# Stores on another queue, tiles in other memory and a new order at the start of SwiGLU in a one-core transformer layer

## The chip, the cores and the metric

The kernel runs on one core of a Trainium2 chip. The metric is the device time of one execution in microseconds, as the median of several runs. A core has TensorE (PE in the profile, PEld its weight loads), VectorE (DVE), ScalarE (ACT), GpSimd (POOL) and SyncE (SP). Here SP does nothing but issue DMA transfers, in the order of its program; a transfer whose condition isn't met holds those behind it.

## The reference

One layer over 2048 latent tokens and 256 context tokens of width 1024, in float32:

```python
h = modulate(rms_norm(x, g0), shift, scale)           # and the same for ctx
q, k, v, r, gate = split(h @ w_in)                    # gated linear attention, 4 heads, both directions
o = scan_forward(q, k, v, gate) + scan_backward(q, k, v, gate)   # the state starts from ctx
x = x + m2 * rms_norm((head_rms_norm(o) * silu(r)) @ w_out, g1)
h = modulate(rms_norm(x, g2), m3, m4)
a, b = split(h @ ffn_w_in)                            # 2 x 2816 columns
x = x + m5 * rms_norm((silu(a) * b) @ ffn_w_out, g3)
```

## The kernel before

Every float32 matmul is made of three: an operand is split into a high part (a cast on ACT or DVE) and a low part (a subtraction on DVE), and hi x hi, hi x lo and lo x hi are summed in PSUM. The work runs through four stages on TensorE.

**Projections and forward scan (0 to about 808 us).** In groups of 512 tokens the projections q, k, v, r are written to DRAM, while the chunks of 128 tokens before them run through the scan (`gla_stages`). Tb, the state that the context hands to the backward scan, stays in a pool of its own (`tbp`, L67 to L69).

**Backward scan, output projection, second norm (about 809 to 1079 us).** Chunks run from 15 down to 0 through `back(gc)`: b0 loads, and steps the state E (from Tb for chunk 15, L678), b1 adds the backward part and takes the head norm, `on` (L690), b2 transposes and multiplies by silu(r), `rt`, b3 multiplies by w_out (two halves, `py`), b4 takes the norm of y, adds x, stores `l1_d` (L754) and keeps the normed rows `xh`. `load_wo` stages the output weights in a buffer `wof` (L644). With four chunks ready, `h2_units` transposes and modulates them to `hf` and makes the operands of SwiGLU: groups 3 and 1 store theirs as they are (L769); groups 2 and 0 come after them and, for each of four blocks k, load two stored blocks (`bl`, L775, L776), make two more and form four sums, each stored to `T_d` (L778 to L787). The sums of group 2 are on POOL, those of group 0 on DVE. The four units of group 0 are run after the loop (L846, L847).

**Features (about 1079 to 1945 us).** SwiGLU's products are done in 2 x 2 blocks with seven products instead of eight (P1 to P7): operands T of P1 to P7, weight blocks and their sums, and results that are summed again. `load_T` (L855) loads one T tile in four parts and splits each; P1, P2 and P6 lie in pool `hL` on the left of memory, the others in `hR` on the right, where the second stage's pool `sq` (bl, y, xh, hf) was until `p2t.close()`. There are 44 features of the two halves p = 1 and 0: 2 x 22. A `Feat` loads its weights wg and wu (L903, L906), and `product` splits a weight block into `whl` (8 buffers) and runs 12 matmuls (L951) into PSUM X (P1, P6, P5, P3), Y (P2) or Z (P7, P4). In step t of the loop (L998) P1, P2, P6 and P7 of feature t and P5, P4 and P3 of feature t-1 are run. `store` puts results into `S_d`, `combine` forms four more results for each pair. Beside it, `w2_units` loads blocks of the output weights (`wl`, six loads for a pair) and stores sums of them to `W_d`. All loads and all stores are on SP (`st = nc.sync`, L38).

**Output (1955 to 2383 us).** `out_group` runs the seven products again: activations `ar` from `S_d` (L1026), weights `wr` from `W_d` or, raw, from w2 (`wraw`, L1036), each in a ring of 14, first for p = 1, then for p = 0.

What sets the order: the program lists the work; when it is built, a planner goes through it in program order and puts next on each engine's queue what it holds to be ready. The order on a queue is then fixed. A pool opened where another was closed reuses its bytes; with `reuse_waits="tile"` a new tile waits for the old tiles that it overlaps, and for no others.

```python
    for u in pend:
        u()
    p2t.close()
    hR = p3.enter_context(tc.tile_pool(name="hR", bufs=1, reuse_waits="tile", side="right"))
```

Of the kernel before, what the change touches and what calls it, by code (L numbers as in the profile page):

```python
# [34 lines left out]
def trunk(ctx, tc, x, cx, modw, cols, rows, consts, wqkr, wv, wvg, wgate, wout, w1, w2, out):  # L35
# [17 lines left out]
    qb_d = [dram.tile([128, H, 128], F32, name=f"qb_d{c}") for c in range(NC_)]  # L53

# [120 lines left out]
    Tf = gp.tile([128, H, DV], F32, name="Tf")  # L175
    glt = [c1.tile([128, 128], F32R, name=f"glt{i}") for i in range(4)]
# [177 lines left out]
    def gla_stages(g, i, c, first):  # L354
# [26 lines left out]
        def s1():  # L381
            e["ks"], e["qs"] = [], []
            for z in range(2):
# [250 lines left out]
    p2t = ExitStack()  # L634
    sp = p2.enter_context(tc.tile_pool(name="sp", bufs=2, reuse_waits="tile"))
# [14 lines left out]
    def back(gc):  # L650
# [13 lines left out]
        def b0():  # L664
# [22 lines left out]
        def b1():  # L687
            op = e["op"]
            ss = sp.tile([128, H], F32, name="ssh", tag="ssh", bufs=3)
            on = sp.tile([128, H, DV], F32, name="on", tag="on", bufs=2)  # L690
# [51 lines left out]
        def b4(xhs):  # L742
# [11 lines left out]
            st.dma_start(out=l1_d[gc], in_=y)  # L754
# [4 lines left out]
    def h2_units(g, xhs):  # L759
# [11 lines left out]
        def second(k):  # L771
# [21 lines left out]

    order = list(range(NC_ - 1, -1, -1))
# [4 lines left out]
    load_wo(range(0, 4), c2, c2)  # L799
# [23 lines left out]
    for i, gc in enumerate(order):  # L823
# [12 lines left out]
        if gc % 4 == 0:  # L836
            pend += h2_units(gc // 4, xhs[gc // 4][::-1])
    p2.close()
    pT.close()
# [3 lines left out]
    p3 = ExitStack()  # L843
# [7 lines left out]
    hR = p3.enter_context(tc.tile_pool(name="hR", bufs=1, reuse_waits="tile", side="right"))  # L851
    ps3z = p3.enter_context(tc.tile_pool(name="ps3z", bufs=1, space=PSUM, reuse_waits="tile", side="right"))
    T = {}

    def load_T(p, i):  # L855
        pool = hL if i in (P1, P2, P6) else hR
# [138 lines left out]
    for i in CHAIN:  # L995
        load_T(1, i)
# [193 lines left out]
```

## Time and profile before

| | us |
|---|---|
| median of 3 runs | 2390.48 |
| lowest, highest | 2389.45, 2391.05 |
| the profiled execution, its own time | 2384.77 |
| its span, first to last instruction | 2383.0 |
| TensorE busy in the span | 2302.0 |

The profile has the engines' instructions with their start and length, what ended an engine's idle time before an instruction, and the DMA transfers. A matmul's length overlaps that of the next. PEclk is the granted clock of TensorE as a share of 2.4 GHz. SPq rows are DMA issues of SP; the length of a merged row (x4) reaches from the first to the last.

### The profile page before, as it was taken

The page shows a single profiled execution, that of the slowest core. Times are in us where ns is not written, and L with a number is a line of the kernel's source. Part 1 is how long each engine was busy: PE and PEld are TensorE (multiplying, and loading weights), DVE is VectorE, ACT ScalarE, POOL GpSimd, SP SyncE. Part 2 cuts the span into 40 slices and gives each one's busy share as a digit, 9 for nine tenths or more (in the row PEclk, how much of TensorE's full clock was granted, in tenths as well). Part 3 has the DMA queues.
Part 4 walks back from the last instruction along what each step waited for, and adds up shares of the span by engine and source line. Part 5 has one row for each costly group of instructions (what it writes and reads, how often), then busy time and mean ns, then how long its engine had stood idle before and what let it go on. Part 6 is the DMA issues. An engine that isn't in the chain of part 4 may idle for free.

```text
span 2383.0 us, 32426 instructions
## 1 busy us (share of the span) xinstructions
PE 2302.0 (97%) x11546; PEld 1939.9 (81%) x11546; DVE 1557.7 (65%) x2478; ACT 1068.8 (45%) x1947; POOL 186.6 (8%) x274
## 2 busy tenths in 40 slices
PE   8999999999998999897999999999999989999998
PEld 4898898898898878685888888888888868888887
DVE  6756666766658576658776666866666647466554
ACT  3535445445547544335433333533333336554552
POOL 1100000000001033631000000000000000001001
PEclk9999999999999999997999999999999999999999
DMA  8765468565455587758787332633233248559655
GB/s 299 225 208 173 148 197 285 177 210 208 153 191 191 206 274 257 243 186 309 258 264 259 125 111 93 230 102 115 97 106 107 75 149 284 191 192 330 201 181 177
DMA packets 228902, 463.98 MB, mean 195 GB/s; under 512 B 22530, under 2 KB 66178, under 8 KB 228740
## 3 DMA queue, kind: packets, MB, share of 16 engines
q1 hardware_dynamic: 228740, 461.92, 57.3%
q8 instruction: 90, 1.47, 0.3%
q14 instruction: 72, 0.59, 0.1%
HBM read 331.27 MB, written 130.56 MB: 194 GB/s over the span
## 4 chain that ended last, share of the span: by engine, by line
PE 52%; DMA 0%; DVE 0%; SPq 0%; ACT 0%; issue 0%; POOLq 0%; POOL 0%; ACTq 0%
PE X L951 20%; PE Z L951 10%; PE X L1074 10%; PE W L1074 8%; PE Y L951 5%; DMA wraw<-w 0%; DMA T<-T_d 0%; DMA T_d<-hf 0%; DVE sa L984 0%; DVE bl L781 0%; DVE y L1055 0%; SPq L906 0%; DVE t L781 0%; DVE hf L781 0%; DVE a L974 0%
## 5 line engine op out<-in xcount | busy, mean ns | idle before, releaser
L951 PE MATMUL X<-T,whl 128*128 128x512 f32 x2112 | 495.7, 390 | 8.2 <-ACT whl L933 7.1
L951 PEld LDWEIGHTS X<-T,whl 128*128 128x128 f32 x2112 | 396.6, 188 | 91.5 <-ACT whl L933 7.5
L951 PE MATMUL Z<-T,whl 128*128 128x512 f32 x1056 | 256.2, 391 | 9.1 <-ACT T L861 9.1
L1074 PE MATMUL X<-wr,ar 128*128 128x512 f32 x1056 | 242.3, 391 | 10.6 <-ACT wr L1038 10.6
L1074 PEld LDWEIGHTS X<-wr,ar 128*128 128x128 f32 x1056 | 199.2, 189 | 52.8 <-ACT wr L1038 11.1
L951 PEld LDWEIGHTS Z<-T,whl 128*128 128x128 f32 x1056 | 199.3, 189 | 51.6 <-ACT T L861 9.5
L86 PE MATMUL pj<-hhi,whi 128*128 128x512 f32 (+1 forms) x544 | 213.6, 395 | 2.1 <-DVE hhi L75 1.4
L87 PE MATMUL pj<-hlo,whi 128*128 128x512 f32 (+1 forms) x544 | 211.4, 389 | 0.0
L88 PE MATMUL pj<-hhi,wlo 128*128 128x512 f32 (+1 forms) x544 | 210.4, 387 | 0.0
L73 ACT CAST whi<-wf 128x1024 fp32r<-128x1024 f32 x104 | 109.0, 1048 | 192.7 <-PE pj L87 84.4
L1028 DVE TENSOR_TENSOR ar<-ar 128x512 fp32r<-128x512 f32 x154 | 106.2, 691 | 131.1 <-ACT ar L1027 130.6
L76 DVE TENSOR_TENSOR wlo<-wf,whi 128x1024 fp32r<-128x1024 f32 x104 | 126.8, 1220 | 86.5 <-ACT whi L73 81.0
L1074 PE MATMUL W<-wr,ar 128*128 128x512 f32 x792 | 180.5, 389 | 0.0
L1074 PEld LDWEIGHTS W<-wr,ar 128*128 128x128 f32 x792 | 148.7, 188 | 30.8
L1027 ACT CAST ar<-ar 128x512 fp32r<-128x512 f32 x154 | 95.5, 621 | 154.6 <-DMA ar<-S_d 107.0
L86 PE MATMUL pj<-whi,hhi 128*128 128x256 f32 x432 | 125.0, 289 | 6.3 <-DVE gs L292 4.9
L951 PE MATMUL Y<-T,whl 128*128 128x512 f32 x528 | 127.7, 390 | 0.0
L87 PE MATMUL pj<-wlo,hhi 128*128 128x256 f32 x432 | 123.2, 285 | 2.8 <-DVE wlo L76 2.8
L88 PE MATMUL pj<-whi,hlo 128*128 128x256 f32 x432 | 122.7, 284 | 0.0
L87 PEld LDWEIGHTS pj<-hlo,whi 128*128 128x128 f32 x544 | 103.5, 190 | 21.3 <-DVE hlo L76 2.2
L86 PEld LDWEIGHTS pj<-hhi,whi 128*128 128x128 f32 x544 | 103.1, 191 | 21.5 <-DVE hhi L75 1.6
L88 PEld LDWEIGHTS pj<-hhi,wlo 128*128 128x128 f32 x544 | 103.4, 190 | 19.7
(231 smaller groups left out, 4273.7 us busy)
## 6 DMA issues: line engine op xcount, KB each, us to landing
ar<-S_d SPq DMA_DIRECT2D x154, 256.0 KB, 3.0
wf<-wqkr SPq DMA_DIRECT2D x68, 512.0 KB, 3.9
wg<-w SPq DMA_DIRECT2D x44, 512.0 KB, 3.5
wu<-w SPq DMA_DIRECT2D x88, 256.0 KB, 2.7
S_d<-sa SPq DMA_DIRECT2D x88, 256.0 KB, 2.0
wr<-W_d SPq DMA_DIRECT2D x88, 256.0 KB, 3.0
wf<-wv SPq DMA_DIRECT2D x36, 512.0 KB, 3.8
wl<-w SPq DMA_DIRECT2D x66, 256.0 KB, 3.7
```

The costliest lines, as they stand in the source:

```text
L73: nc.scalar.copy(out=hi, in_=src)
L76: nc.vector.tensor_sub(out=lo, in0=src, in1=hi.bitcast(F32))
L86: nc.tensor.matmul(out=ps, lhsT=ahi, rhs=bhi, start=start, stop=False)
L87: nc.tensor.matmul(out=ps, lhsT=ahi, rhs=blo, start=False, stop=False)
L88: nc.tensor.matmul(out=ps, lhsT=alo, rhs=bhi, start=False, stop=stop)
L951: nc.tensor.matmul(out=ps, lhsT=w[:, a, ks], rhs=t[:, k, b, :], start=first and k == 0 and n == 0, stop=k == 3 and n == 2, skip_group_chec ...
L1027: nc.scalar.copy(out=t[:, 0, :], in_=raw)
L1028: nc.vector.tensor_sub(out=t[:, 1, :], in0=raw, in1=t[:, 0, :].bitcast(F32))
L1074: nc.tensor.matmul(out=po[j], lhsT=a[:, x, 128 * j:128 * j + 128], rhs=w[:, z, :], start=first and fp == 0 and n == 0, stop=fp == NFP - 1 ...
```

## The change

1. **Queues.** These stores go from SP's queue to POOL's: all of features (`S_d`) and weight sums (`W_d`), the y of chunks 1 and 0 (`l1_d`), and those of group 0's units to `T_d`.
2. **Memory.** Tb lies among the scan's tiles, is scaled at the last chunk and goes through DRAM (`Tb_d`) to E. The staging of the first four output weights shares the buffers of `on`. T of P1 has a pool `hG` of its own below the second stage's pools; the feature weights' pool w3 lies directly above it, then hL with P2, P6, P7 and P5; only P4 and P3 are on the right, with g1, sa and wl. a1 has 3 buffers instead of 4. In the output stage the rings are cut in two: 4 slots of `ar` lie where T of P1 was, 10 of `wr` above, the rest behind; the two sets of PSUM banks lie on either side.
3. **Order.** T of P1 is loaded in the loop of chunks. Features 0 and 1 start together: P1 P1 P2 P2, then P6 P7 P5 of feature 0 and P6 of feature 1, each followed by one of group 0's four units, then the rest. Z of feature 0 takes a buffer of X.
4. **Output weights.** A pair takes four loads of w2 instead of six.

```diff
+    Tb_d = dram.tile([128, D], F32, name="Tb_d")
-    pT = ExitStack()
-    tbp = pT.enter_context(tc.tile_pool(name="tbp", bufs=1))
-    Tb = tbp.tile([128, H, DV], F32, name="Tb")
...
+    Tb = gp.tile([128, H, DV], F32, name="Tb")
...
                     if gc == NC_ - 1:
                         put_fb(gc, lnDb[:, NC_, :, 1])
+                        for h in range(H):
+                            nc.scalar.activation(out=Tb[:, h, :], in_=Tb[:, h, :], func=AF.Copy, scale=fb[:, gc, h:h + 1])
+                        st.dma_start(out=Tb_d, in_=Tb.rearrange("p h v -> p (h v)"))
...
+    p3 = ExitStack()
+    hG = p3.enter_context(tc.tile_pool(name="hG", bufs=1, reuse_waits="tile"))
     sp = p2.enter_context(tc.tile_pool(name="sp", bufs=2, reuse_waits="tile"))
...
-            w = spool.tile([128, D], F32, name="wof", tag="xt2", bufs=2)
+            w = spool.tile([128, D], F32, name="wof", tag="on" if spool is sp else "xt2", bufs=2)
...
-                for h in range(H):
-                    nc.scalar.activation(out=E[0][:, h, :], in_=Tb[:, h, :], func=AF.Copy, scale=fb[:, gc, h:h + 1])
+                sync.dma_start(out=E[0].rearrange("p h v -> p (h v)"), in_=Tb_d)
...
-            st.dma_start(out=l1_d[gc], in_=y)
+            (nc.gpsimd if gc < 2 else st).dma_start(out=l1_d[gc], in_=y)
...
-            st.dma_start(out=Td[P3][k], in_=b22)
+            (st if g > 1 else nc.gpsimd).dma_start(out=Td[P3][k], in_=b22)
...
-                st.dma_start(out=Td[i][k], in_=out)
+                (st if g else nc.gpsimd).dma_start(out=Td[i][k], in_=out)
...
+    T, T_pool = {}, {P1: hG}
...
-    load_wo(range(0, 4), c2, c2)
+    load_wo(range(0, 4), c2, sp)
...
             pend += h2_units(gc // 4, xhs[gc // 4][::-1])
+        if gc == 3:
+            load_T(1, P1)
     p2.close()
...
+    w3 = p3.enter_context(tc.tile_pool(name="w3", bufs=2, reuse_waits="tile"))
     hL = p3.enter_context(tc.tile_pool(name="hL", bufs=1, reuse_waits="tile"))
-    w3 = p3.enter_context(tc.tile_pool(name="w3", bufs=2, reuse_waits="tile"))
...
-    for u in pend:
-        u()
-    p2t.close()
...
+    T_pool.update({i: hL for i in (P2, P6, P7, P5)})
+
+    def w2_units(fp):
+        b = {}
+
+        def load():
+            for j, nn in ((0, 0), (0, 1), (1, 0), (1, 1)):
+                b[j, nn] = hR.tile([128, 512], F32, name="wl", tag="wl", bufs=4)
+                sync.dma_start(out=b[j, nn], in_=w2[fp + NFP * j, :, 512 * nn:512 * nn + 512])
+
+        def sums(*what):
+            for i, out, x, y, op in what:
+                nc.vector.tensor_tensor(out=b[out], in0=b[x], in1=b[y], op=op)
+                nc.gpsimd.dma_start(out=W_d[i][fp], in_=b[out])
...
-                self.Z = ps3z.tile([128, GT], F32, name="Z", tag="Z", bufs=2)
+                if self.f == 0 and self.p == 1:
+                    self.Z = ps3.tile([128, GT], F32, name="Z", tag="X", bufs=3)
+                else:
+                    self.Z = ps3z.tile([128, GT], F32, name="Z", tag="Z", bufs=2)
...
-                self.a1 = o3.tile([128, GT], F32, name="a1", tag="a1", bufs=4)
+                self.a1 = o3.tile([128, GT], F32, name="a1", tag="a1", bufs=3)
...
-            st.dma_start(out=S_d[self.p][i][self.f % NFP], in_=t)
+            nc.gpsimd.dma_start(out=S_d[self.p][i][self.f % NFP], in_=t)
...
-    for i in CHAIN:
+    n = len(seq)
+    feats = {0: Feat(*seq[0]), 1: Feat(*seq[1])}
+    for i in (P2, P6, P7, P5):
         load_T(1, i)
-    n = len(seq)
-    for t in range(n + 1):
+    for j, i in ((0, P1), (1, P1), (0, P2), (1, P2)):
+        feats[j].product(i)
+    for j, i in ((0, P6), (0, P7), (0, P5), (1, P6)):
+        feats[j].product(i)
+        pend.pop(0)()
+    p2t.close()
+    hR = p3.enter_context(tc.tile_pool(name="hR", bufs=1, reuse_waits="tile", side="right"))
+    ps3z = p3.enter_context(tc.tile_pool(name="ps3z", bufs=1, space=PSUM, reuse_waits="tile", side="right"))
+    T_pool.update({P4: hR, P3: hR})
+    for i in (P4, P3):
+        load_T(1, i)
+    done = {(1, i) for i in CHAIN}
+    for j, i in ((1, P7), (1, P5), (0, P4), (0, P3), (1, P4), (1, P3)):
+        feats[j].product(i)
+    for t in range(2, n + 1):
...
-    r4 = p4.enter_context(tc.tile_pool(name="r4", bufs=1, reuse_waits="tile"))
+    rA = p4.enter_context(tc.tile_pool(name="rA", bufs=1, reuse_waits="tile"))
     y4 = p4.enter_context(tc.tile_pool(name="y4", bufs=1, reuse_waits="tile"))
-    ps4 = p4.enter_context(tc.tile_pool(name="ps4", bufs=1, space=PSUM, reuse_waits="tile"))
+    rB = p4.enter_context(tc.tile_pool(name="rB", bufs=1, reuse_waits="tile"))
+    rC = p4.enter_context(tc.tile_pool(name="rC", bufs=1, reuse_waits="tile"))
+    ps4 = {"W": p4.enter_context(tc.tile_pool(name="ps4", bufs=1, space=PSUM, reuse_waits="tile")),
+           "X": p4.enter_context(tc.tile_pool(name="ps4x", bufs=1, space=PSUM, reuse_waits="tile", side="right"))}
...
+    def slot(tag):
+        i = count[tag] % 14
+        count[tag] += 1
+        first, nf = {"ar": (rA, 4), "wr": (rB, 10)}[tag]
+        pool, sfx, nb = (first, "", nf) if i < nf else (rC, "2", 14 - nf)
+        return pool.tile([128, 2, 512], F32R, name=tag, tag=tag + sfx, bufs=nb)
...
-        t = r4.tile([128, 2, 512], F32R, name=tag, tag=tag, bufs=14)
+        t = slot(tag)
...
-        raw = r4.tile([128, 512], F32, name="wraw", tag="wraw", bufs=4)
+        raw = rB.tile([128, 512], F32, name="wraw", tag="wraw", bufs=4)
```

## Rows read from the trace of the kernel before

**Rows 1.** The page, part 1, the whole span: engine, busy us, share, instructions.

```profile
PE 2302.0 (97%) x11546; PEld 1939.9 (81%) x11546; DVE 1557.7 (65%) x2478; ACT 1068.8 (45%) x1947; POOL 186.6 (8%) x274
```

**Rows 2.** Waits of PE, whole span: total us, times, longest.

```profile
PE X L1074 <- ACT wr L1038: 10.6, 1, 10.6
PE Z L951 <- ACT T L861: 9.1, 1, 9.1
PE X L951 <- ACT whl L933: 7.1, 1, 7.1
```

**Rows 3.** Windows: busy per engine (x instructions), clock, DMA share, GB/s; first row L951 alone.

```profile
1078.70:1955.20 876.50, 843.29 (x3696) 695.30 (x3696) 0.98 0.47 157
...
1078.70:1117.80 39.10, 21.38 (x92) 17.09 (x92) 31.18 (x49) 19.01 (x34) 4.91 (x7) 0.75 0.90 312
1055.00:1078.70 23.70, 23.68 (x112) 19.16 (x110) 11.95 (x18) 10.27 (x22) 8.54 (x10) 1.00 0.66 228
1130.00:1940.00 810.00, 810.00 (x3575) 670.71 (x3574) 534.30 (x837) 307.24 (x538) 0.00 (x0) 1.00 0.43 145
...
1115.00:1120.00 5.00, 2.14 (x4) 1.29 (x5) 4.22 (x7) 2.62 (x5) 0.00 (x0) 0.50 0.98 341
```

**Rows 4.** Timeline of PE, first crossing: start, us, line, operation, idle before.

```profile
1078.29 0.39 PE L88 MATMUL py<-wo_hi,olo 128*128 128x512 f32 x1
1085.76 1.22 PE L951 MATMUL X<-T,whl 128*128 128x512 f32 x2 [7.09 <-ACT whl L933]
...
1091.13 4.67 PE L102 MATMUL tp<-ident,xh 128*128 128x128 f32 x24 [0.52 <-DVE xh L95]
...
1117.86 5.21 PE L951 MATMUL Z<-T,whl 128*128 128x512 f32 x12 [9.08 <-ACT T L861]
```

**Rows 5.** Timeline of SP's queue (DMA issues), first crossing.

```profile
1071.18 1.87 SPq L860 DMA_DIRECT2D T<-T_d  x4
1077.59 0.32 SPq L754 DMA_DIRECT2D l_d<-y  x1
...
1079.80 0.43 SPq L903 DMA_DIRECT2D wg<-w  x1
...
1113.01 9.81 SPq L860 DMA_DIRECT2D T<-T_d  x16
```

**Rows 6.** Timeline of DVE, first crossing.

```profile
1083.96 1.41 DVE L751 SCALAR_TENSOR_TENSOR y<-py,ry,A 128x512 f32<-128x512 f32 x2 [0.44 <-POOL ry L82]
...
1110.14 0.69 DVE L781 TENSOR_TENSOR bl<-bl,t 128x512 f32<-128x512 f32 x1
```

**Rows 7.** Groups of DVE from 1078.7 to 1111: busy us, mean ns, idle before.

```profile
L862 DVE TENSOR_TENSOR T<-T 128x512 fp32r<-128x512 f32 x10 | 6.3, 682 | 0.0
```

**Rows 8.** The chain that ended last, in order of time: start, us, work.

```profile
1142.19 2.72 PE Y L951 x12
...
1955.23 31.92 PE X L1074 x132
1987.15 29.92 PE W L1074 x132
```

**Rows 9.** Timeline of all engines, second crossing.

```profile
1941.70 2.88 PE L951 MATMUL X<-T,whl 128*128 128x512 f32 x12
...
1946.70 1.77 SPq L979 DMA_DIRECT2D S_d<-sa  x3
...
1949.06 0.41 SPq L1026 DMA_DIRECT2D ar<-S_d  x1
```

**Rows 10.** Groups of POOL, whole span.

```profile
L753 POOL TENSOR_TENSOR y<-y,xt 128x1024 f32<-128x1024 f32 x15 | 36.7, 2450 | 23.0 <-DVE y L751 18.9 <-DMA xt<-x 4.1
...
L781 POOL TENSOR_TENSOR hf<-hf,hf 128x512 f32<-128x512 f32 x4 | 5.8, 1454 | 0.3
```

**Rows 11.** The page, part 6: DMA issues, KB each, us to landing.

```profile
S_d<-sa SPq DMA_DIRECT2D x88, 256.0 KB, 2.0
```

**Rows 12.** Waits of PE from 800 to 870 us.

```profile
PE tp L722 <- DVE on L703: 3.0, 3, 2.1
```

More of the change, by code (lines that the diff above doesn't have):

```diff
@@ L689, in b1 @@
             ss = sp.tile([128, H], F32, name="ssh", tag="ssh", bufs=3)
-            on = sp.tile([128, H, DV], F32, name="on", tag="on", bufs=2)
+            on = sp.tile([128, D], F32, name="on", tag="on", bufs=2).rearrange("p (h v) -> p h v", h=H)
             for hh in range(2):
@@ L792, in h2_units, with load_T @@
         return [lambda k=k: second(k) for k in range(4)]
+    T, T_pool = {}, {P1: hG}
+    def load_T(p, i):
+        t = T_pool[i].tile([128, 4, 2, GT], F32R, name=f"T{i}", tag=f"T{i}", bufs=1)
+        for k in range(4):
+            raw = t[:, k, 1, :].bitcast(F32)
+            sync.dma_start(out=raw, in_=T_d[p][i][k])
+            nc.scalar.copy(out=t[:, k, 0, :], in_=raw)
+            nc.vector.tensor_sub(out=t[:, k, 1, :], in0=raw, in1=t[:, k, 0, :].bitcast(F32))
+        T[i] = t
     order = list(range(NC_ - 1, -1, -1))
@@ L850, in trunk @@
-    p2t.close()
[L851 to L856, printed above, removed]
-        t = pool.tile([128, 4, 2, GT], F32R, name=f"T{i}", tag=f"T{i}", bufs=1)
-        for k in range(4):
-            raw = t[:, k, 1, :].bitcast(F32)
-            sync.dma_start(out=raw, in_=T_d[p][i][k])
-            nc.scalar.copy(out=t[:, k, 0, :], in_=raw)
-            nc.vector.tensor_sub(out=t[:, k, 1, :], in0=raw, in1=t[:, k, 0, :].bitcast(F32))
-        T[i] = t
@@ L865, in w2_units @@
-    def w2_units():
-        hold = {}
-        def wl(fp, half, n):
-            t = o3.tile([128, 512], F32, name="wl", tag="wl", bufs=3)
-            sync.dma_start(out=t, in_=w2[fp + NFP * half, :, 512 * n:512 * n + 512])
-            return t
-        def sub(i, fp, x, y, op=ALU.subtract):
-            nc.vector.tensor_tensor(out=x, in0=x, in1=y, op=op)
-            st.dma_start(out=W_d[i][fp], in_=x)
-            return x
-        def t1(fp):
-            sub(P5, fp, wl(fp, 0, 1), wl(fp, 0, 0))
-        def t3(fp):
-            b12 = wl(fp, 0, 1)
-            b22 = wl(fp, 1, 1)
-            hold[0] = sub(P7, fp, b22, b12)
-        def t2(fp):
-            b11 = wl(fp, 0, 0)
-            hold[0] = sub(P6, fp, b11, hold[0], ALU.add)
-        def t4(fp):
-            sub(P4, fp, wl(fp, 1, 0), hold[0])
-        return [lambda fp=fp, t=t: t(fp) for fp in range(NFP) for t in (t1, t3, t2, t4)]
@@ L895, in trunk @@
-    units = w2_units()
+    T_pool.update({i: hL for i in (P2, P6, P7, P5)})
[9 more added lines that the diff above has]
+                nc.gpsimd.dma_start(out=W_d[i][fp], in_=b[out])
+        return [load, lambda: sums((P7, (1, 1), (1, 1), (0, 1), ALU.subtract), (P5, (0, 1), (0, 1), (0, 0), ALU.subtract)),
+                lambda: sums((P6, (0, 0), (0, 0), (1, 1), ALU.add)), lambda: sums((P4, (1, 0), (1, 0), (0, 0), ALU.subtract))]
@@ L897, in trunk @@
+    units = [u for fp in range(NFP) for u in w2_units(fp)]
     class Feat:
@@ L971, in product @@
             else:
-                g1 = o3.tile([128, GT], F32, name="g1", tag="g1", bufs=1)
+                g1 = hR.tile([128, GT], F32, name="g1", tag="g1", bufs=1)
                 nc.scalar.activation(out=g1, in_=ps, func=AF.Silu)
@@ L1002, in trunk @@
             j = t - lag
-            if not 0 <= j < n:
+            if not j < n or (j, i) in done:
                 continue
@@ L1007, in trunk @@
                 load_T(0, i)
-        if units:
-            units.pop(0)()
-        if t >= 2 and t % 2 == 0:
+        for _ in range(2 if t == 4 else 1):
+            if units:
+                units.pop(0)()
+        if t % 2 == 0:
             feats[t - 1].combine(feats[t - 2])
@@ L1034, in w2_block @@
         half, nn = {P1: (0, 0), P2: (1, 0), P3: (1, 1)}[i]
-        raw = r4.tile([128, 512], F32, name="wraw", tag="wraw", bufs=4)
+        raw = rB.tile([128, 512], F32, name="wraw", tag="wraw", bufs=4)
         sync.dma_start(out=raw, in_=w2[fp + NFP * half, :, 512 * nn:512 * nn + 512])
-        t = r4.tile([128, 2, 512], F32R, name="wr", tag="wr", bufs=14)
+        t = slot("wr")
         nc.scalar.copy(out=t[:, 0, :], in_=raw)
@@ L1059, in out_group @@
         lo, hi = slice(0, 512), slice(512, 1024)
-        X = [ps4.tile([128, 512], F32, name="X4", tag=tx, bufs=4) for j in range(4)]
+        X = [ps4[tx].tile([128, 512], F32, name="X4", tag=tx, bufs=4) for j in range(4)]
         y0 = [y4.tile([128, D], F32, name="y0", tag="y0", bufs=6) for j in range(4)]
@@ L1067, in out_group @@
             if i in (P2, P7):
-                W = [ps4.tile([128, 512], F32, name="W4", tag=tw, bufs=4) for j in range(4)]
+                W = [ps4[tw].tile([128, 512], F32, name="W4", tag=tw, bufs=4) for j in range(4)]
             po = W if i in (P2, P7, P4) else X
```

6 lines of the change are left out of this document (2 added, 4 removed).

## The prediction

> **What bounds the kernel now.** Busy shares come first: TensorE is busy for 97% of the span [rows 1], so a change pays only where it stands still or runs slowly. The list of who waited for whom names the places: three waits of 10.6, 9.1 and 7.1 us, each a single one [rows 2]. All lie where stages meet. Inside the feature stage, from 1130 to 1940 us, TensorE is busy for all 810 us at full clock, DVE for 534, POOL for none, and the DMA share is 0.43 [rows 3]. The reader should see that nothing in those 810 us can be won, only lost.
>
> The crossings are priced from windows. The 876.5 us from 1078.7, where the attention projection ends [rows 4], to 1955.2, where the output stage starts, hold 3696 matmuls [rows 3]. A product of 12 takes 2.72 us [rows 8], so 308 products need 837.8. The 32 transposes in the stretch need about 4 (24 took 4.67 at half clock [rows 4]). That leaves 34.7 us lost: 10.6 in the second crossing and so 24.1 in the first. There 39.1 us contain 17.7 of standstill, and the mean clock is 0.75 [rows 3]. Behind the 9.1 us wait the granted clock is 0.50, 1.2 GHz [rows 3], and the first product takes 5.21 us instead of 2.72 [rows 4]. The output stage starts likewise: 31.92 against 29.92 us for 132 matmuls [rows 8], 2.0 more.
>
> The queues say who is late. SP issues in order. After four T loads at 1071.18 it stands until 1077.59, when the store of y goes out, which waited for POOL's sum; only at 1079.80 comes wg, the first feature weights [rows 5], and TensorE starts at 1085.76 [rows 4]. Four of the seven T tiles have their memory on the right, where the operand sums live: the last sum ends at 1110.83 [rows 6], the T loads follow at 1113.01 [rows 5], and TensorE goes on at 1117.86 [rows 4]. At the second crossing the last product starts at 1941.70, the sums' stores leave SP at 1946.70 and the first load of the output stage at 1949.06 [rows 9], although what it reads was stored hundreds of us before.
>
> **The first crossing after the change.** Three parts act together. The y stores of the last two chunks and all 20 stores of the last operand sums go to POOL, so SP stands no longer before wg. The weights lie where buffers of the backward stage end early, and T of P1 has memory of its own, so both can be loaded and split before 1078.7, while DVE is at half load (11.95 of 23.7 us [rows 3]). The new order then gives TensorE two P1 products at once, which cover the loads of the next T tiles, and ten products before anything needs the right side. The 7.1 us wait goes with its half-clock tail. New waits come:
> - Y's bank is freed by the projection's last scaling, which ends at 1085.4 [rows 6]; two P1 products end at 1078.7 + 5.4 = 1084.1. Cost 1.3.
> - Y has one buffer, and two P2 products now follow each other: DVE must take the first away, one sum of 0.69 [rows 6] and its handshake. Cost 1.
> - T of P4 still waits for the last operand sum. DVE now has 16 T splits there, where before it had 10 [rows 7]: 6 x 0.69 = 4.1, and two weight splits more, 1.4; four splits for the first two features move ahead of 1078.7, minus 2.8. The last sum so ends near 1113.5. Store, T load and split took 7.0 from the last sum to the product; I add 1 for POOL. TensorE could start P4 at about 1121.
>
> Until then it has 10 products and the transposes: 27.2 + 4 + 2.3 of waits reach 1112.2. T of P3 needs only the memory of xh and y, free earlier, so the planner may put both P3 products first: 1117.6. Stall 3.4 to 8.8, middle 6, then 2 for half clock. Loss left: 2.3 + 8 = 10.3 of 24.1, a gain of **13.8**. Bounds: 5 if the sums slip by 9 us more (the old wait of 9.1 once more), 21 if feature 2 fills the gap.
>
> What is queued behind a POOL store? Norm factors, and y sums of earlier chunks. The last y's store waits for the same sum as the norm behind it, so it holds nobody. A store on POOL has no row. From below: free, with the landing of 2.0 us that SP's store has [rows 11]. From above: a POOL pass over a tile twice its size, 2.45 us [rows 10]. I take a pass over the same size, 1.45 [rows 10], since POOL has to write the transfer out itself.
>
> **The feature stage.** 198 stores (154 of features, 44 of weight sums) leave SP for POOL, which is idle there; 22 loads of 256 KB go. At a DMA share of 0.43 that is worth nothing to TensorE. One a1 buffer goes: each lives for some two features of 7 x 2.72 = 19 us, and three suffice. Four combinations share three sa buffers, so the fourth waits for the first's store; 1.45 us more on DVE, idle for a third of the stage, is hidden. Cost 0; the bound above is rival 4.
>
> **The second crossing.** SP has no stores left in the stage, so A5, the rings' first loads and the raw weights wait for memory alone. The first four activation slots lie on T of P1; nine products, 24.5 us, follow the last P1. Raw weights and weight slots lie on T of P2, P6 and P7, all read before the last three products, 8.2 us. The first output product then follows the last feature product directly; of its PSUM banks on the right two are free and two were Z's. Gain 10.6 + 2.0, less 1 for an evacuation in the way: **11.6**. Bounds: 6 if the splits come late, 12.6.
>
> **The start of the backward stage.** Tb is scaled earlier and goes through DRAM: one store and one load of 512 KB more, four ACT instructions moved. The staging of the first output weights shares buffers with "on"; its second pair of loads could hold the first head norm. But these buffers lie on the scan's gate tiles, free before the scan ends, so the loads can start earlier than before. TensorE waits 3.0 us for "on" here now [rows 12]. I take 0, between minus 3 (that wait gone) and plus 3 (doubled).
>
> Sum: 13.8 + 11.6 = 25.4. The profiled execution took 2384.8 (span 2383.0 and 1.8 around it), so 2359.4; it ran 5.7 below the median of 2390.5, against which I forecast 2390.5 - 25.4 = **2365**.
>
> **A rule against it.** SP stood from about 1073 to 1077.6 before a store [rows 5]: the order of the queue cost these 4.5 us, and issuing did not. The Trainium skill's "DMA: Bandwidth & Descriptors", section "Issuing engines are not separate DMA queues", says that transfers from several engines share the same DMA engines, and that a second issuer saves only sequencer time, usually small. By that rule the moved stores would give almost nothing in the first crossing; the trace agrees that the DMA engines are nearly full there, at 0.90 [rows 3], but not that issue time is all that was lost.
>
> **Rivals.**
> 1. The first crossing is bound by transfers. At a share of 0.90 over 39.1 us, T tiles (6 MB), sums (7 MB) and weights move no faster from another queue; DVE too is busy for 31.2 of them [rows 3]. For it: the same bytes have to pass. Against it: the 4.5 us in which SP stood, and T of P1 and the weights of two features, which move ahead. Gain there 2 to 3 instead of 13.8: 2376. This is where that page's rule leads. Chance 0.13.
> 2. The second crossing stays: the planner still puts the rings' loads last, or a slot overlaps a late reader. For it: before, T of P1 was free by 1920 too, and yet its memory was loaded at 1949 [rows 9]. Against it: then 198 stores stood on that queue. Gain 13.8 only: 2377. Chance 0.11.
> 3. Feature 2 covers the rest of the first crossing: gain 21 + 12.6, 2357. Chance 0.07.
> 4. Slower: POOL's stores set the pace of the feature stage. Its 838 us over 198 stores are 4.23 us each. From 4.23 on, a0, a1 and sa come free too late, DVE blocks and TensorE waits for splits; from 4.36 on the 25 us won are gone. At 5 us: 198 x 0.77 = 152, less 25: 2517. Against it: 4.23 is three times the row I took and above the higher bound of 2.45. Chance 0.06. The Trainium skill's "SBUF — State Buffer", section "SBUF: two separate sides", warns that a store from POOL's queue cannot write its descriptors while DVE runs in a two-port mode; no run here shows such a store.
> 5. The change does nothing visible: other waits take the place of both. 2388. Chance 0.03.
>
> **How the numbers follow.** The forecast has 0.60, with a range of its own of 2355 to 2373. The range of 2352 to 2379 takes in rivals 1 to 3 and leaves out 4, 5 and tails. About 0.2% (4.8 us) can be told from no change. Faster: 0.60, 0.11 of rival 1, 0.11 and 0.07: 0.89. Same: 0.02 of rival 1 and 0.03: 0.05. Slower: 0.06.
>
> **What would show it.** Right: no wait above 1.5 us between 1079 and 1112; wg and T of P1 issued before 1078; a wait of 3 to 9 us at the first P4 or P3; ar and raw weights issued before the last feature product; no long wait at the output stage's first matmul and its first 132 in 29.9 us; TensorE at 100% between. Wrong: waits in the feature stage after 1150 (rival 4), a T of P2 that lands after 1085 (rival 1), ar behind the end of the features (rival 2), or more than 6 us of new waits between 800 and 850.

## The result and the profile after

The change made the kernel slower: 2422.15 us median against 2390.77 in the same comparison, ratio 1.0128 (95% interval 1.0111 to 1.0146). The forecast was 2365. The profiled execution took 2423.08 us, its span 2421.3, which is 38.3 more than before. That is more than the 31.4 between the medians, since the profiled execution of before was 5.7 us below its median.

The page, part 1, and from part 3 the queue of POOL's stores (packets, MB, share of 16 engines' span), kernel after:

```profile
PE 2323.6 (96%) x11546; PEld 1948.2 (80%) x11546; DVE 1558.7 (64%) x2478; ACT 1067.6 (44%) x1947; POOL 307.1 (13%) x494
...
q0 software_dynamic: 17728, 58.21, 6.6%
```

Against [rows 1], TensorE has as many matmuls and is busy 21.6 us longer: part of them ran at the lower clock, and part of those in the output stage at a slower pace (below). POOL has 220 instructions more, which are the moved stores; they are a queue of their own now, 58 MB. The list of waits of PE shows new names on top, and the three waits of [rows 2] are gone or short:

```profile
PE X L939 <- DVE a L954: 17.5, 4, 7.0
PE tp L725 <- DVE on L706: 11.3, 6, 8.0
...
PE X L939 <- DVE y L754: 3.5, 1, 3.5
...
PE X L1089 <- DVE wr L1054: 2.5, 1, 2.5
```

The timeline of PE says where they lie:

```profile
839.07 1.12 PE L725 MATMUL tp<-ident,on 128*128 128x128 f32 x4 [8.04 <-DVE on L706]
...
1096.50 2.93 PE L939 MATMUL X<-T,whl 128*128 128x512 f32 x12
1102.92 1.70 PE L939 MATMUL X<-T,whl 128*128 128x512 f32 x4 [3.50 <-DVE y L754]
...
1151.85 6.52 PE L939 MATMUL Z<-T,whl 128*128 128x512 f32 x15 [1.71 <-ACT T L804]
...
1220.26 2.88 PE L939 MATMUL X<-T,whl 128*128 128x512 f32 x12
1227.58 5.49 PE L939 MATMUL X<-T,whl 128*128 128x512 f32 x12 [4.43 <-DVE a L954]
...
1277.39 4.59 PE L939 MATMUL X<-T,whl 128*128 128x512 f32 x12 [6.99 <-DVE a L954]
...
1986.77 0.49 PE L1089 MATMUL X<-wr,ar 128*128 128x512 f32 x1 [1.19 <-ACT wr L1053]
1989.77 31.85 PE L1089 MATMUL X<-wr,ar 128*128 128x512 f32 x131 [2.50 <-DVE wr L1054]
2021.45 30.43 PE L1089 MATMUL W<-wr,ar 128*128 128x512 f32 x132
```

From such timelines each profile can be cut into stages. "Backward" runs from the scan's last matmul to the projection's last. "First crossing" is the time from there to the start of the 21st product, less 20 x 2.72 and 4 for the transposes; "features" what the other 288 products took beyond 2.72 each; "second crossing" the time from the last product's end to the third output matmul, less the 0.4 of two matmuls; "output" the rest.

| us | before | after | difference | fastest version (below) |
|---|---|---|---|---|
| scan, until | 808.8 | 812.5 | +3.7 | 808.6 |
| backward | 269.7 | 284.0 | +14.3 | 274.3 |
| first crossing, lost | 24.1 | 21.8 | -2.3 | 15.4 |
| features, lost | 0.0 | 25.3 | +25.3 | 0.0 |
| second crossing, lost | 11.7 | 4.3 | -7.4 | 4.3 |
| output | 426.4 | 431.2 | +4.8 | 429.4 |

The differences sum to 38.4. The reader should see that both crossings did become shorter and that three other stages pay for it. The scan's end is not read: it lies between 808.6 and 816.2 in the profiles below, though none of the edits made there touches the scan. Whether the change itself, which scales Tb in the scan, costs something there is not shown.

### The profile page after: what moved, and what is told of

It reads as the page before. It is cut to its first block, busy times and chain, and to the rows that moved or that the text cites. A ratio compares the mean times of both kernels' runs of the same rounds, so it can differ in the third digit from the quotient of the medians.

```text
span 2421.3 us, 32503 instructions
## 1 busy us (share of the span) xinstructions
PE 2323.6 (96%) x11546; PEld 1948.2 (80%) x11546; DVE 1558.7 (64%) x2478; ACT 1067.6 (44%) x1947; POOL 307.1 (13%) x494
## 4 chain that ended last, share of the span: by engine, by line
PE 47%; issue 6%; POOL 5%; DVE 3%; DMA 2%; ACT 1%; SPq 0%; POOLq 0%; ACTq 0%; DVEq 0%
PE X L939 16%; PE X L1089 10%; PE Z L939 8%; PE W L1089 7%; PE Y L939 4%; POOL y L756 1%; POOL W_d L875 1%; DMA T<-T_d 1%; DVE rt L727 1%; POOL S_d L967 0%; DVE y L754 0%; DVE op L700 0%; DMA rt<-r_d 0%; PE py L85 0%; DVE ohi L73 0%
## 5 line engine op out<-in xcount | busy, mean ns | idle before, releaser
L939 PE MATMUL X<-T,whl 128*128 128x512 f32 x2112 | 504.0, 394 | 22.5 <-DVE a L954 17.5
L85 PEld LDWEIGHTS pj<-hlo,whi 128*128 128x128 f32 x544 | 103.9, 191 | 21.6 <-DVE hlo L74 2.3
L86 PEld LDWEIGHTS pj<-hhi,wlo 128*128 128x128 f32 x544 | 103.8, 191 | 19.7
```

The costliest lines, as they stand in the source:

```text
L85: nc.tensor.matmul(out=ps, lhsT=ahi, rhs=blo, start=False, stop=False)
L86: nc.tensor.matmul(out=ps, lhsT=alo, rhs=bhi, start=False, stop=stop)
L939: nc.tensor.matmul(out=ps, lhsT=w[:, a, ks], rhs=t[:, k, b, :], start=first and k == 0 and n == 0, stop=k == 3 and n == 2, skip_group_chec ...
```

## Experiments

Each ratio is to runs of the kernel before on the same chip; differences of 3 or 4 us between two of them are inside their intervals.

### The feature stage: queue or bundle

First what is late there. The timeline of DVE, kernel after:

```profile
1224.30 0.69 DVE L874 TENSOR_TENSOR wl<-wl 128x512 f32<-128x512 f32 x1 [4.68 <-DMA wl<-w]
1224.91 0.68 DVE L919 TENSOR_TENSOR whl<-wu,whl 128x512 fp32r<-128x512 f32 x1
1225.51 1.41 DVE L874 TENSOR_TENSOR wl<-wl 128x512 f32<-128x512 f32 x2
1226.84 0.68 DVE L954 TENSOR_TENSOR a<-a,X 128x512 f32<-128x512 f32 x1
```

DVE stands 4.68 us for a load of output weights; behind it in its fixed order is the sum that empties a bank of PSUM (L954), and at 1227.58 TensorE goes on. Behind the three longer of the four waits TensorE runs at 1.2 GHz for some 5 us: the product above takes 5.49 instead of 2.88, and the windows view of after gives 0.50 as granted clock there (last but two columns) and 0.95 over all 200 us:

```profile
1160.00:1360.00 200.00, 182.51 (x771) 149.12 (x771) 134.91 (x215) 63.04 (x112) 42.63 (x79) 0.95 0.59 204
...
1228.00:1233.00 5.00, 5.00 (x13) 3.83 (x13) 4.42 (x8) 2.14 (x4) 1.08 (x2) 0.50 0.93 313
```

That makes the 25.3: 17.5 of waits and some 8 at the lower clock. The load is late because its buffer is still being stored. Waits of SP's queue, 1160 to 1310 us, kernel after:

```profile
SPq L870 <- DMA W_d<-wl: 65.6, 35, 7.1
```

Two things changed there: the store's queue, and the unit, which now loads four blocks into the four buffers that the unit before is storing.

```diff
 # e2_wsum_sp (after, with)
-                nc.gpsimd.dma_start(out=W_d[i][fp], in_=b[out])
+                st.dma_start(out=W_d[i][fp], in_=b[out])
```

> The changed kernel, but only the 44 stores of weight sums go back to the SyncE queue. Theory Q (the queue): the four weight loads of a unit wait for stores of the unit before, which land late from POOL's queue; DVE stands up to 5.7 us on those loads and TensorE behind it, 17.5 us in four waits between 1223 and 1303 plus some 8 us at half clock. Then the waits go: 2396 to 2402. Theory B (the bundle): four loads at once into four buffers that are all still being stored are late from either queue: 2418 to 2426.

Measured: 2401.2 us, ratio 1.0047 (1.0029 to 1.0064): theory Q, and the features lose 4 instead of 25.3. Waits of PE, 1160 to 1310 us, and then those of SP:

```profile
PE X L939 <- DVE a L954: 1.9, 1, 1.9
```

```profile
SPq L870 <- DMA W_d<-wl: 12.6, 17, 2.0
```

```diff
 # e3_units (after, with the units of before, stores from POOL, four buffers)
-    units = [u for fp in range(NFP) for u in w2_units(fp)]
+    units = [lambda fp=fp, t=t: t(fp) for fp in range(NFP) for t in (t1, t3, t2, t4)]
```

> The changed kernel, but the weight sums are made as in the kernel before, in units of one or two loads each (66 loads, not 44), in four buffers, stores still from POOL. Theory B (the bundle): DVE's waits become short again (before: 21 waits, longest 3.6 us, TensorE none) and the four waits of TensorE go: 2396 to 2403. Theory Q (the queue): stores from POOL hold the buffers just as long, waits stay: 2417 to 2428.

Measured: 2415.7, ratio 1.0111 (1.0089 to 1.0134). TensorE's waits stay at 16.0 us in four, the loads wait 81.6 us at SP for stores. DVE's single waits did become short, as the theory of the bundle said, but they are more, and TensorE stands all the same (waits of DVE, 1160 to 1310 us):

```profile
DVE wl L873 <- DMA wl<-w: 44.5, 29, 3.5
```

So it is the queue and not the bundle; the theory of the bundle has fallen. The reverse test puts the moved stores alone onto POOL's queue in the kernel before:

```diff
 # e6_before_pool (before, with)
-            st.dma_start(out=S_d[self.p][i][self.f % NFP], in_=t)
+            nc.gpsimd.dma_start(out=S_d[self.p][i][self.f % NFP], in_=t)
 # likewise W_d, l1_d of chunks 1 and 0, and T_d of group 0's units
```

> The kernel before with nothing changed but the queue: the stores that the change moves go to POOL. Theory: the weight sums, with three buffers there, wait for stores from the other queue and TensorE for them, some 20 us in the feature stage; the second crossing gains up to 10: 2396 to 2412. Rival: before, memory sets both crossings, and the queue alone costs and brings nothing: 2387 to 2393.

Measured: 2406.4, ratio 1.0067 (1.0053 to 1.0082). TensorE waits for the same sum (10.2 us in two, none before), the features lose 16.4 in all, and the second crossing's wait is 10.9 as before: **the queue alone costs 16 us and brings nothing.** Is it POOL, or any queue that isn't the loads' own?

```diff
 # e7_wsum_act (after, with)
-                nc.gpsimd.dma_start(out=W_d[i][fp], in_=b[out])
+                nc.scalar.dma_start(out=W_d[i][fp], in_=b[out])
```

> The changed kernel, but the 44 stores of weight sums are issued by ScalarE, on a queue that is neither POOL's nor that of the loads. Theory S (POOL's stores as such are late: written out in 0.54 us and landing later): as on SyncE, 2398 to 2405. Theory O (any queue other than that of the loads: stores and the loads behind them share the engines, and the reload waits for the landing): the waits stay, 2416 to 2425.

Measured: 2414.8, ratio 1.0115 (1.0100 to 1.0130), by its interval not to be told from after. Waits of PE and of SP in the stage:

```profile
PE X L939 <- DVE a L954: 11.2, 4, 3.2
```

```profile
SPq L870 <- DMA W_d<-wl: 70.2, 36, 7.5
```

The store's row and its landing (min, median, max) from POOL in after, from SP in e2_wsum_sp, from ACT in e7_wsum_act, 1160 to 1310 us:

```profile
L875 POOL DMA_DIRECT2D W_d<-wl x44: 539/539/542, 1167.1 to 1304.2; - x44
...
DMA to landing us min/median/max: 2.3/3.2/6.4
```

```profile
L875 SPq DMA_DIRECT2D W_d<-wl x44: 319/326/1327, 1165.1 to 1298.1; - x44
...
DMA to landing us min/median/max: 2.0/2.1/4.3
```

```profile
L875 ACTq DMA_DIRECT2D W_d<-wl x44: 326/326/362, 1163.0 to 1294.5; - x44
...
DMA to landing us min/median/max: 2.0/2.3/5.3
```

Most of the loss stays, as theory O said, but the run has a rival of its own that theory O doesn't name. A store that ACT issues stands in ACT's own order and holds what is behind it until the sum is made (waits of ACT, e7_wsum_act, 1160 to 1310 us):

```profile
ACT whl L918 <- DVE wl L874: 35.4, 9, 7.8
ACT g L961 <- DVE wl L874: 20.4, 3, 8.3
```

Little of this reaches the others directly: TensorE waits 2.1 us for ACT there, DVE 2.0. That a queue other than SP's is enough for most of the loss is therefore likely, and not cleanly shown. From POOL the stores land 1 us later than from SP (median), and TensorE waits 17.5 us for the sum, against 11.2 with the stores on ACT.

How the lateness comes about is seen only in part. From the last sum of a unit to the last reload of its buffers it takes 5.0 us in after, 3.9 with ACT's stores, 3.3 with SP's (means of ten units, from the starts in the trace). But it takes 4.5 with all stores on SP (e5_all_sp, below), where the features lose nothing, so this time doesn't decide by itself. DVE, whose order was fixed when the kernel was built, stands for these loads 42.7, 35.6 and 24.1 us in about ten waits each. Nor does that sum decide, or the length of one wait: the kernel before has nearly as much and TensorE waits for none of it, and in after a wait of 3.5 us at 1247.8 reaches TensorE at once, while behind one of 5.7 at 1261.6 TensorE runs on until 1277.39. Waits of DVE, before and after:

```profile
DVE wl L874 <- DMA wl<-w: 37.5, 21, 3.6
```

```profile
DVE wl L874 <- DMA wl<-w: 42.7, 10, 5.7
```

SP stands long in both cases: 65.6 us ahead of the reloads in after, and in e2_wsum_sp 64.5 ahead of the stores and 12.6 ahead of the reloads. That the planner's order allows for the store when it shares the reload's queue, and too little when it doesn't, is argued from this and was not tried by itself. The Trainium skill's "DMA: Bandwidth & Descriptors", section "Issuing engines are not separate DMA queues", says that a second issuer saves only sequencer time; e6_before_pool agrees about the gain, and shows a cost of 16 us beside it.

### The start of the backward stage

Timelines of ACT and then of DVE, kernel after, ahead of the wait of 8.04 us:

```profile
834.52 1.04 ACT L71 CAST wo_hi<-wof 128x1024 fp32r<-128x1024 f32 x1 [1.59 <-DMA wof<-wout]
835.47 0.41 ACT L703 ACTIVATE on<-op 128x256 f32<-128x256 f32 x1
```

```profile
835.60 1.23 DVE L74 TENSOR_TENSOR wo_lo<-wof,wo_hi 128x1024 fp32r<-128x1024 f32 x1 [1.41 <-ACT wo_hi L71]
838.66 1.14 DVE L706 TENSOR_SCALAR on<-op,rh 128x256 f32<-128x256 f32 x4 [1.83 <-POOL rh L80]
```

In ACT's order the head norm (L703) stands directly behind the cast of the fourth staged weight, though its input was ready at 827.3. It takes the two buffers of the four weights by turns, so its own was the third's, split by 834.2; the split of the fourth, which the expectation below names, ends at 836.8, after the norm has begun.

```diff
 # e1_wof (after, with)
+        own = hG.tile([128, 4, D], F32, name="wof", tag="T0", bufs=1) if spool is sp else None
-            w = spool.tile([128, D], F32, name="wof", tag="on" if spool is sp else "xt2", bufs=2)
+            w = own[:, k, :] if spool is sp else spool.tile([128, D], F32, name="wof", tag="xt2", bufs=2)
```

> The changed kernel, but the first four output weights are staged in the memory that the first T tile gets later, four buffers of their own instead of the two head-norm buffers. Theory: the head norm (on, 835.5 us) waited for the last split of the staging (ended 836.8) and TensorE for it, 8.0 us, with a stretch at half clock behind it; with buffers of its own the norm comes as early as before, and the run takes 2409 to 2413 us instead of 2422. Rival: transfers set the start of the backward stage (DMA share 0.9 there), and the norm is late anyway: 2419 to 2424.

Measured: 2412.6, ratio 1.0087 (1.0072 to 1.0102). The loads leave at 803.6 instead of 817.9 (before: 813.7), the norm ends 7 us earlier, and the wait is 1.09; the stage takes 274.1 instead of 284.0. The edit gives the weights both buffers of their own and an earlier start, and does not tell the two apart. Timelines of SP, after and then e1_wof, and of PE, e1_wof:

```profile
817.94 0.90 SPq L649 DMA_DIRECT2D wof<-wout  x2
```

```profile
803.57 1.76 SPq L650 DMA_DIRECT2D wof<-wout  x4
```

```profile
831.64 0.70 PE L726 MATMUL tp<-ident,on 128*128 128x128 f32 x4 [1.09 <-DVE on L707]
```

### The output stage

Its groups of 132 matmuls take up to 30.43 us by the rows above (before: 30.08) at full clock and without a wait. Consecutive matmuls start 226.7 ns apart, but 233.3 on the first 4 of the ring's 14 slots: those whose activation tile is in rA and whose weight tile is in rB. The weight tile starts 82624 bytes after its activation tile there, by the sizes of the pools between them; all other pairs, and all of before, are a multiple of 4096 apart.

```diff
 # e4_pad (after, with)
+    pd = p4.enter_context(tc.tile_pool(name="pd", bufs=1))
+    pd.tile([128, 16], F32, name="pd")
     rB = p4.enter_context(tc.tile_pool(name="rB", bufs=1, reuse_waits="tile"))
```

> The changed kernel, but the memory of the weight ring starts 64 bytes later, so that activation and weight tiles of every ring slot start at the same offset modulo 128 bytes. In the changed kernel 4 of 14 slots differ by 64 there, and matmuls on them start 233.5 ns apart instead of 226.7. Theory: the offset does it; all slots run at 226.7, 4 us less, 2418. Rival: the slots are slow for where they lie or for what is loaded beside them: 2422, the same four slots at 233.5.

Measured: 2417.3, ratio 1.0105 (1.0089 to 1.0120); but for single ones, and for the start of the stage at the lower clock, the matmuls start 226.7 ns apart, and the groups (timeline of PE) are as before. The interval of the ratio overlaps that of after, so it is the starts that show the gain. It is 3.4 of the 4.8 us: the rest lies in the first group, which runs longer at the lower clock, and behind the last matmul.

```profile
2019.97 30.08 PE L1091 MATMUL W<-wr,ar 128*128 128x512 f32 x132
```

Whether the offset or the place does it was tried on the fastest version (c5_half, below), with other amounts of padding:

> The fastest version (feature stores split by half) with the weight ring 96 bytes later instead of 64: activation and weight tiles of the first four slots then start 32 apart modulo 128 bytes. Theory (offset modulo 128 has to be equal): these slots run at 233.5 ns a matmul again, 473 or so slow ones. Rival (only a difference of 64 is slow, or moving the ring was enough): all at 226.7.

> The same with 128 bytes: the ring has moved, and the start offsets differ by 64 modulo 128 as in the changed kernel. Theory: slow again, 233.5 ns on four of 14 slots, output stage 4 us longer. Rival (it was the place of the ring, not the offset): all at 226.7.

f1_pad96: 2383.0, the four slots at 233.3. f2_pad128: 2378.4, at 228.9, so the modulus of 128 has fallen. Next the distance modulo 256:

> The weight ring 256 bytes later, so that the distance from an activation tile to its weight tile in the first four slots is 82880 bytes, 192 more than a multiple of 256, as in the changed kernel (82624). So far: 82624 slow (233.3 ns a matmul), 82688 fast (226.7), 82720 slow (233.3), 82752 nearly fast (228.9). Theory D (the distance modulo 256 decides, and 0 is fast): 233.3 again. Rival: no such period, any value between.

> The weight ring 320 bytes later: distance 82944, a multiple of 256 like 82688. Theory D: 226.7 on all slots. Rival: slower again, and 64 bytes were a lucky place.

f3_pad256: 2383.3, at 233.3. f4_pad320: 2376.4, at 226.7 on all slots. (These four are single runs; their claim rests on the matmuls' starts.)

| padding, bytes | distance | modulo 256 | ns a matmul, first 4 slots |
|---|---|---|---|
| 0 | 82624 | 192 | 233.3 |
| 64 | 82688 | 0 | 226.7 |
| 96 | 82720 | 32 | 233.3 |
| 128 | 82752 | 64 | 228.9 |
| 256 | 82880 | 192 | 233.3 |
| 320 | 82944 | 0 | 226.7 |

Six of six fit. The place of the weight tile alone is not what decides: slots 5 to 13, with weight tiles in the same pools, run at 226.7 in all of these runs (on slot 4 the first few matmuls are slow too, in after and f3_pad256). Only the values 0 and 192 were tried twice, so the period of 256 rests on these two pairs; why it is so is open.

### Together, and the crossings

```diff
 # c1_three = e1_wof + e2_wsum_sp + e4_pad
```

> The changed kernel with the three edits together: staging of the first output weights in buffers of its own, weight-sum stores on the SyncE queue, weight ring 64 bytes later. Theory: the three losses lie at different places and add: 2422 less 10, 21 and 5 is 2386, a little faster than the kernel before (2390). Rival: one loss covers another (a stage that starts earlier meets the same transfers): 2391 to 2400.

Measured: 2389.2, ratio 0.9994 (0.9985 to 1.0004): 3 us above the sum of the parts, and together about what the change lost. Left are the first crossing, where c1_three loses 20.8, some 6 us of the backward stage, and 4.2 in the features (one wait of 2.4 us and the clock behind it).

```diff
 # c2_sums_first (c1_three, with)
-    for j, i in ((0, P1), (1, P1), (0, P2), (1, P2)):
+    for j, i in ((0, P1), (1, P1)):
         feats[j].product(i)
-    for j, i in ((0, P6), (0, P7), (0, P5), (1, P6)):
+    while pend:
+        pend.pop(0)()
+    for j, i in ((0, P2), (1, P2), (0, P6), (0, P7), (0, P5), (1, P6)):
         feats[j].product(i)
-        pend.pop(0)()
```

> The three edits together, and the last operand sums stand ahead of the first P2 products instead of between the later ones. Theory O (order): in the changed kernel the transposes for these sums wait behind products and come in four pieces, and the last sum ends 47 us after the attention projection (before: 32); in one piece they end 10 us or more earlier, the wait for T of P4 and the half clock behind it go: 5 to 9 us less than the three edits alone. Rival T (transfers and DVE): the sums are bound by their loads, stores and by DVE's splits, and the order only moves the waits: within 2 us of the three edits alone.

Measured: 2388.8, ratio 0.9992 (0.9982 to 1.0003); first crossing 20.8 as without. The last transposes for the sums do come earlier, some 26 us after the projection instead of 35, and yet the last sum ends 46.9 us after it. The order is not it; the wait for T becomes one for a weight split (5.0 us).

```diff
 # c3_T_sp (c1_three, with)
-            (st if g > 1 else nc.gpsimd).dma_start(out=Td[P3][k], in_=b22)
+            st.dma_start(out=Td[P3][k], in_=b22)
-                (st if g else nc.gpsimd).dma_start(out=Td[i][k], in_=out)
+                st.dma_start(out=Td[i][k], in_=out)
```

> The three edits together (2389), and the stores of the last operand sums back on the SyncE queue too; feature stores stay on POOL's. Theory Q (a store on POOL's queue delays whoever reloads its buffer): the sums' buffers come free earlier, T of P4 too, and the first crossing shortens as it did with all stores on SyncE (waits of 8.5 us there instead of 13): 2383 to 2386. Rival: that crossing depends on order and DVE only: 2388 to 2391.

Measured: 2381.8, ratio 0.9973 (0.9961 to 0.9984); first crossing 15.8. The features lose 3.8 less too, since the wait of 2.4 us is not there; why that one went is open. ACT's waits from 1070 to 1160 us show what came free earlier, in c1_three and then in c3_T_sp:

```profile
ACT hf L101 <- DMA T_d<-hf: 3.5, 3, 2.7
ACT hf L101 <- DMA T_d<-t: 2.8, 2, 1.6
```

```profile
ACT hf L101 <- DMA T_d<-hf: 1.0, 2, 0.6
```

ACT waits 6.3 us for buffers that are being stored from POOL, and 1.0 where they are stored from SP; the last sum ends 42.5 us after the projection instead of 47.8. (In e6_before_pool, too, the last sum came later than in the kernel before, 39.5 us after the projection against 32.2.) Then all stores on SP, without and with the two other edits:

```diff
 # e5_all_sp (after; S_d, W_d, l1_d and T_d all)
-nc.gpsimd.dma_start(
+st.dma_start(
 # c4_sp_three = e5_all_sp + e1_wof + e4_pad
```

> The changed kernel with all stores back on the SyncE queue, the rest as changed. Theory: the weight-sum stores were the loss of that part (21 us), and the feature stores on POOL's queue are what lets the output stage's loads start early (second crossing: 3.7 us of waits now, 10.6 before); so the second crossing becomes longer by some 7 us and the run takes about 2408. Rival: the second crossing is short because of the memory alone: 2400 to 2402, as with the weight-sum stores alone moved back.

> All stores on the SyncE queue (2396), with the staging buffers of their own and the ring 64 bytes later: without any of the queue part. Theory: 2396 less 10 and 5 is 2381 to 2383, faster than the kernel before by some 8 us, with the wait of 7.8 us at the second crossing still there. Rival: as with the three edits, part of it is lost: 2386 to 2391.

e5_all_sp: 2396.4, ratio 1.0025 (1.0016 to 1.0034), faster than the 2408 expected and than e2_wsum_sp: the first crossing loses 15.1, the features nothing. The second crossing did grow, but by 4.1 us of waits (7.82 against 3.69) and not by 7 (timelines of PE and SP): the first loads of ar still leave early, and only the raw weights stand behind three stores.

```profile
1962.50 32.68 PE L1089 MATMUL X<-wr,ar 128*128 128x512 f32 x132 [7.82 <-ACT wr L1053]
```

```profile
1930.23 1.75 SPq L1041 DMA_DIRECT2D ar<-S_d  x4
...
1956.79 1.77 SPq L967 DMA_DIRECT2D S_d<-sa  x3
1958.67 2.02 SPq L1051 DMA_DIRECT2D wraw<-w  x4
```

c4_sp_three: 2383.1, ratio 0.9976 (0.9967 to 0.9986): what is left of the change without its queue part (memory, order and four loads of w2, which were not tried apart) is worth 6 us, once the two slips of memory are mended. By the losses of the stages, then, the one place where POOL's queue pays is the second crossing, and the last version uses it there alone:

```diff
 # c5_half (c3_T_sp, with l1_d from st, and)
-            nc.gpsimd.dma_start(out=S_d[self.p][i][self.f % NFP], in_=t)
+            (st if self.p else nc.gpsimd).dma_start(out=S_d[self.p][i][self.f % NFP], in_=t)
```

> As before, but feature stores go from the SyncE queue in the first half of the features, where weight sums and the first crossing share the transfers, and from POOL's in the second half, ahead of the second crossing; weight sums, operand sums and y go from SyncE. Theory: both gains together, no wait on a sum in the feature stage and only 3.7 us at the second crossing: 4 us less than all on SyncE, 2377 to 2380. Rival: the short second crossing came from the whole stage's stores, or the gain is lost elsewhere: 2381 to 2386.

Measured: **2378.6**, ratio 0.9963 (0.9950 to 0.9976), faster than both kernels. Its interval overlaps those of c3_T_sp and c4_sp_three. The stages show what it has over c4_sp_three: the second crossing loses 4.3 instead of some 9. They show next to nothing over c3_T_sp, whose feature stores are all on POOL's queue and whose features lose 0.4, so that the split by halves is not shown to matter. No wait is left in the features; the crossings' rows in the waits of PE:

```profile
PE X L940 <- DVE y L755: 3.4, 1, 3.4
...
PE Z L940 <- ACT T L805: 3.1, 1, 3.1
...
PE X L1092 <- DVE wr L1057: 2.5, 1, 2.5
```

## Why the prediction was wrong, step by step

- **The feature stage (forecast 0, measured 25.3).** This is the step that decided the sign. The sentence that failed says that the stores "leave SP for POOL, which is idle there": it asked what a store costs POOL, and nothing about who reuses the stored buffer. POOL's price was even overstated (1.45 taken, 0.54 measured), and its pace never mattered. What mattered is the four buffers of weight sums, stored 44 times, that a load on SP's queue fills again: with these 44 stores alone back on SP the features lose 4 (e2_wsum_sp). The reload came late, DVE stood for it, and TensorE behind DVE; that it came later than DVE's fixed order allowed for is argued. Rival 4 named the symptom (DVE blocks, TensorE waits) with the wrong cause and a price that would have needed 4.36 us a store.
- **The start of the backward stage (forecast 0, bounds minus 3 and plus 3, measured +14.3).** The prediction saw the sharing and argued it away: "these buffers lie on the scan's gate tiles, free before the scan ends, so the loads can start earlier than before". They started at 817.9 (before: 813.7), and with buffers of their own at 803.6. The bound was a doubled wait; it should have been the time of four staged weights. Buffers of their own give back 9.9; some 5 us of the stage stay in all versions. In e1_wof they are many short waits of TensorE, 19.7 us in the stage against 15.2 before; what makes them is open.
- **The first crossing (forecast gain 13.8, bounds 5 and 21, measured 2.3).** The early loads did what was said: TensorE goes from the projection to the first product without a gap at 1096.50, and the waits of 7.1 and 9.1 us are gone. The point in time that failed is "The last sum so ends near 1113.5", 35 us after the projection; it ended 47.1 after it (before: 32). That is 12 us later than forecast, where the lower bound allowed for 9 (timeline of DVE, kernel after, the sum that ends last):

```profile
1142.96 0.68 DVE L784 TENSOR_TENSOR bl<-bl,t 128x512 f32<-128x512 f32 x1
```

  "I add 1 for POOL" is the part that runs put a number on: the stores from POOL cost 5 (c3_T_sp), since buffers and loads wait for them. From SP the gain is 8 to 9, inside the bounds. The wait for the late T, though, is 1.7 us where the forecast had a stall of 6, since TensorE had 12 products to run before it and not 10. The terms of the loss that failed are the two beside it: the other waits (forecast 2.3, measured 11.5) and the lower clock (forecast 2, some 8.5 by what is left of the 21.8). Of these waits 4.2 are for weight splits behind ACT, which had stood 3.5 us at 1137.81 for a buffer still being stored. Also missed: the second P1 product waits 3.5 us for the projection's last scaling; the forecast had put that on Y's bank with 1.3. Rival 1 gave 2 to 3 for this crossing and was right in size; its reason, that the same bytes must pass, explains the rest only in part, since the same bytes from SP pass 5 us sooner.
- **The second crossing (forecast 11.6, bounds 6 and 12.6, measured 7.4).** Right in mechanism: ar leaves at 1961.13 and the raw weights at 1966.57, long before the last product. What is left, 3.7 us, is the order of the casts: they had their data, and stood behind the last silu (timeline of ACT, kernel after), which the prediction priced at 1. The 2.0 us of lower clock that it counted as won stayed: the first 131 matmuls of the row above take 31.85 us, where it listed 29.9 as a sign of being right.

```profile
1985.61 0.60 ACT L961 ACTIVATE g<-X 128x512 f32<-128x512 f32 x1 [7.57 <-PE X L939]
1986.11 2.17 ACT L1053 CAST wr<-wraw 128x512 fp32r<-128x512 f32 x4
```

- **The output stage (not forecast, +4.8).** Moving the ring slots was costed as memory that is free or not; that their distance has a price in matmul time was not in the prediction at all.
- **The rule on POOL's stores.** The Trainium skill's "SBUF — State Buffer", section "SBUF: two separate sides", would have POOL's descriptors held up while DVE is in a two-port mode. The row of W_d's stores shows no delay of the issue: 539 to 542 ns for each of 44, beside a DVE that is busy for 134.9 of 200 us. It is no test of the rule, since no row shows which of DVE's instructions run in such a mode; and why these stores land later than SP's (3.2 us against 2.1) no run shows.

Three of the listed signs of a wrong forecast came: waits in the feature stage after 1150, more than 6 us of new waits between 800 and 850, and, for rival 1, a late T of P2. It landed 7.8 to 10.7 us after the projection's end, where the mark of 1085 stands for 6.3.

## What to carry to other kernels

Before a store is moved to another queue, find who fills its buffer next, and which engine's fixed order counts on that load: here the price of the move was there, and not on the engine that issues the store. Move only stores behind which no load fills the buffer again soon, as here the feature stores (c3_T_sp, c5_half). Shared staging buffers are priced by the whole time of what they stage, not by the wait that stands there now.

## What the runs showed of the hardware

- Float32 matmuls of 128x512 in the output stage started 226.7 ns apart where the two operands' start addresses in a partition differ by a multiple of 256 bytes, and 233.3 where they differ by 192 or 32 more, 228.9 at 64 more: 3% on the slots concerned, at a granted clock of 1.00 and without a wait in the profile.
- A store of 256 KB from POOL's queue takes POOL 0.54 us, and SP 0.32 us from its own.
- Behind a wait of 4.43 us TensorE ran some 5 us at a granted clock of 0.50; behind one of 1.61 us, at 1251, the product took 3.02 us, hardly more than the 2.88 at full clock. Four waits of 17.5 us together so cost 25.3.
